# A hybrid trunk layer on one core: long lists of small score products handed to TensorE in pieces of 32, shorter turns of small work, two head pairs split for the output projection at an earlier event

## The chip, the cores and the metric

The kernel runs on one core of one Trainium2 chip. The metric is the device time of one execution in microseconds (us), as the median of three runs. All inputs and the output are fp32.

## The reference

One layer of a decoder trunk, 512 tokens of width 2048 behind 16 learned meta tokens, so T = 528. The input is RMS-normalised and multiplied by one combined projection `w_in`; its columns feed three mixers on separate heads, and the gated outputs go through one output projection `w_out`, a residual and a last RMSNorm. Cut to what matters here:

```python
proj = rms_norm(x, norm_w) @ w_in        # dq dk dv dz db da | gq gk gv gz gl | fq fk fv fz ff
# DeltaNet, 6 heads x 128, chunks of 64: (I + A) sol = rhs, A strictly lower triangular
a_mat = where(strict, einsum('bhncd,bhnsd->bhncs', kb, kc) * decay, 0)
sol = triangular_solve(eye + a_mat, rhs, lower=True)
# GLA, 5 heads (dk 64, dv 128), chunks of 64, a decay for each key dimension:
dec = exp(where(causal, g[i] - g[j], -inf))
attn = einsum('bhid,bhjd,bhijd->bhij', q, k, dec)
o = q_dec @ state + attn @ v
# forgetting attention, 5 heads x 128: softmax(q.k + c_t - c_s) @ v in blocks of 128 queries
out = rms_norm(x + concat(o_dn, o_gla, o_fox) @ w_out, final_norm_w)
```

## The kernel before, in words

**The work.** Every fp32 operand is split into a high and a low part (names ending in h and l, or beginning with h and l: `xh`/`xl`, `hbfz`/`lbfz`), and a product is three matmuls: high by high, low by high, high by low. Four stages follow each other on TensorE (PE). Most of `w_in` is multiplied first, two 128-column blocks at a time by a seven-product scheme (PSUM tiles `px`). Then come the columns of the queries and gates of GLA and of the forgetting attention, one block of 48 heavy matmuls of 512 columns each (`pbgq`, `pbfq`, `pbgz`, `pbfz`); this is the stage in which the three mixers do their own work. Then the output projection: its first part in plain products (`po`, operands `ho` and `lo` from `w_out`, `oh` and `ol` from the heads), its second by the seven-product scheme (`ps`) for the head pairs kp in `STK = (3, 4, 6, 7)`, and last the rest and the norm.

**The order.** Nothing is left to a run-time scheduler. A class `Weave` (from line 235) records the program in one order and pins it on every engine. Every piece of work is a Python generator (a chain) which yields one operation, a list of PE operations, a request for a buffer (`Get`) or events to wait for. `run` keeps a model of each engine's time and takes the chain whose next operation could start first, priority added. A list is emitted whole: nothing comes between its products. On PE a rule of turns stands above this: operations are light (the mixers' small products) or heavy (the projections); a light turn goes on while its modelled time with the next list stays below `LIGHT`, a heavy turn lasts at least `HEAVY`, if the other kind has something ready. A DMA is issued on SP's queue when the modelled DMA time is less than `BACK[t > BT]` ahead; `BACK` has one value for the first 100 us and one for the rest. Since all instructions are emitted by one helper, they all carry its line, L283; tiles tell them apart.

**GLA's score products.** GLA has five heads in three pairs p = 0, 1, 2 (the last has one head). A chunk's lower triangle is computed in levels: `gla_levels` (line 1365) makes, for the groups of levels (64, 32), (16, 8), (4, 2) and (1, 0), one list of products into PSUM tiles `pss` (one for each head of the pair), and yields it in one go. With two heads the lists have 24, 64, 64 and 64 products, with one head half of that. Each fp32 product is two matmuls in the trace, so a list of 64 is 128 matmul records. `level_operands` makes the factors: `gd` from the cumulated gates `ggc` by DVE and an exponential on ACT, then `kx = gkT * gd` and `qx = gqT * gd` on DVE. When a list is done, its masked result is taken over into `a` by DVE (COPY_PREDICATED with the mask `lmk`) and the bank is given back.

**DeltaNet's small products.** `levels` (line 1102) inverts the 64 x 64 triangles of three heads (a group g = 0 or 1) from 32 x 32 blocks: a list of 24 products of `an` and `uc` into `pm`, a copy to `m1`, a list of 48 products of `xc` and `m1`. `xc` is loaded on SP's queue from a scratch tile `sc`; `uc` is its transpose by DVE.

**Other names.** `gst` is GLA's state, `pkd` its products and gkd's transposes; `pfa`, `pfd`, `fp`, `fsm` are scores and probabilities of the forgetting attention, `pfw` its output, whose last product needs `mh` and `ml`, the two parts of a small matrix taken from `pfw` (`ml` by DVE); `pvf` and `pvgv` transpose values that were loaded to `fv` and `vgv`. `kT`, `qT` and `spgq`, `spfq` are DeltaNet's and the others' spilled rows, `rfq`, `rgz`, `rfz` raw weights.

**Head pairs of the output projection.** `seven_heads` (line 1740) splits the two finished heads of pair kp in `STK` into parts and forms their sums; it waits for `e_d`, the end of the mixers' work, unless kp is in `EARLY_KP`, where it waits for the end of GLA (`e_gla`) and the finished head 10 and takes its buffers from the pool `w_s` or `d_s`. `seven_operands` (line 1816) splits the weights for the same products.

Of the kernel before, what the change touches and what calls it, by code (L numbers as in the profile page):

```python
# [8 lines left out]
F32 = mybir.dt.float32  # L9
# [9 lines left out]
P = 128  # L19
D = 2048  # L20
KT = D // P
NM = 16
S = 512
# [5 lines left out]
NN = NB * H  # L29
# [52 lines left out]
STP, IP = 0.0, 0.05  # L82
GP, KX = (), 5
AP, KA, XP, GAP = -0.2, 2, 0.3, 0.1
BACK, BT = (3.0, 1.5), 100.0
LIGHT, SLACK, DMAL, STL = 2.0, 0.25, 1.1, 2.5
HEAVY, NEAR = 1.5, 0.05
KW = 2
NXP, SQP, NSL = -0.6, 0.0, 1.5
LP, LSL = 0.1, 1.0  # L90
WP, AOP, HDP = 1.0, -0.6, 0.0
EARLY_KP = ()
STK, KOS, OS0, OSN, OSP = (3, 4, 6, 7), 3, 1, 2, 0.1


# [265 lines left out]
def tile_hybrid_trunk(ctx, tc, xT, xtok, mtok, w_gate, w_first, w_in, w_out, consts, lmask, fin_w, out):  # L361
# [3 lines left out]
    V, A, G, PE, SP = (Engine(k, e) for k, e in zip("VAGPS", (nc.vector, nc.scalar, nc.gpsimd, nc.tensor, nc.sync)))  # L365
# [165 lines left out]
    zs, spill = {}, {}  # L531
    dzs = [drp.tile([H, P, S], F32, name=f"dzs{g}") for g in range(2)]
    e_sp, e_bank = {}, {}
    sp_of = lambda key: e_sp.setdefault(key, Ev())

    def silu_row(z, key, dst):
        if key[0] == "dz" or key in EARLY:
            yield A.activation(z, z, AF.Silu)
            yield SP.dma_start(out=dst, in_=z)
            return  # L540
        t = yield Get(row_s, f"st{key[0]}{key[1]}")
        yield V.tensor_scalar_max(t[:, :S], z, LOW)
        yield A.activation(t[:, :S], t[:, :S], AF.Exp, scale=-1.0)
        yield A.activation(t[:, :S], t[:, :S], AF.Ln, bias=1.0)
        yield A.activation(t[:, :S], t[:, :S], AF.Exp, scale=-1.0)
        yield VT(out=z, in0=z, in1=t[:, :S], op=ALU.mult)
        row_s.give(t)
        yield SP.dma_start(out=dst, in_=z)
# [174 lines left out]
    def token_rows(key, c, u):  # L723
# [29 lines left out]
    other_pairs = [(("gk", 0), ("gk", 1)), (("gv", 0), ("gv", 1)), (("gv", 2), ("gv", 3)), (("gv", 4), ("gk", 2))] \  # L753
        + [(("fk", h), ("fv", h)) for h in range(FOX_HEADS)]
    PAIRS = [p for c in zip(conv_pairs, other_pairs) for p in c]
    xpart = lambda k0, s: tuple((lambda j, t=t: t[k0 + j][:, s]) for t in (xh, xl))
    tpart = lambda d, s: tuple((lambda j, w=w: d[j // 2][w][:, j % 2, s]) for w in range(2))
    RHS = {1: xpart(0, L), 2: xpart(8, L), 3: xpart(8, R), 4: tpart(tb_, L), 5: tpart(ta, L), 6: tpart(tb_, R),
# [9 lines left out]

    pairs = [Pair(i) for i in range(len(PAIRS))]

# [67 lines left out]
    def store(p, n, u):  # L838
        yield VT(out=u, in0=u, in1=rstd, op=ALU.mult)
        key = p.keys[n]  # L840
        if key[0] in CONV:
            c = yield Get(row_s, f"cv{p.i}{n}")
            yield from conv(u, key, c, u)
            if key[0] != "dv":
                yield spilled(key, c)
            W.go(token_rows(key, c, u), -0.1, f"rows{key[0]}{key[1]}", 3.0)
        else:
            yield spilled(key, u)
            sp_of(key).set()

    CONV = {"dq": 0, "dk": DN_HEADS, "dv": 2 * DN_HEADS}
# [18 lines left out]
    EARLY = [(k[:2], int(k[2])) for k in EORD.split()]  # L870
# [231 lines left out]
    def levels(g):  # L1102
        s = gs[g]
        an, xc, xm, um = s.an, s.xc, s.xm, s.um
        uc = yield Get(m_s, f"uc{g}", (P, NN, 32))
        yield V.transpose(uc.rearrange("p n c -> p (n c)"), xc.rearrange("p n c -> p (n c)"))
        pm = yield Get(bank_s, f"pm{g}")
        p3 = pm[:, : NN * 32].rearrange("p (n c) -> p n c", c=32)
        lh = [(slice(64 * q, 64 * q + 32), slice(64 * q + 32, 64 * q + 64)) for q in range(2)]
        yield [PE.matmul(p3[lo_, n, :], an[hi_, n, lo_], uc[hi_, n, :], start=True, stop=True)  # L1110
               for n in range(NN) for lo_, hi_ in lh]
        m1 = yield Get(m_s, f"m1{g}", (P, NN, 32))
        for q in range(2):
            yield A.copy(m1[64 * q : 64 * q + 32], p3[64 * q : 64 * q + 32])
        W.go(state0(g), 0.0, f"state{g}")
        yield V.transpose(um.rearrange("p h c -> p (h c)"), xm.rearrange("p h c -> p (h c)"))
        e_um[g].set()
        yield [PE.matmul(p3[a, n, :], l[lo_, n, :], r[lo_, n, :], start=True, stop=True)
               for n in range(NN) for lo_, hi_ in lh for a, l, r in ((lo_, xc, m1), (hi_, m1, xc))]
        l1 = yield Get(m_s, f"l1{g}", (P, NN, 32))  # L1120
        yield A.copy(l1, p3)
        bank_s.give(pm)
        m_s.give(m1)
        s.uf = uf = yield Get(big_s, f"uf{g}", (P, NN, P))
        yield G.memset(uf, 0.0)
        for r in range(4):
            c = slice(32 * r, 32 * r + 32)
            yield A.copy(uf[c, :, c], uc[c])
        m_s.give(uc)
        for q in range(2):  # L1130
            yield V.tensor_copy(uf[64 * q : 64 * q + 32, :, 64 * q + 32 : 64 * q + 64], l1[64 * q : 64 * q + 32])
# [233 lines left out]
    def gla_levels(p, group, sets, pair, at, a32, ev):  # L1365
        ne = pair[0]
        ready = evs(*group)
        for s in group:
            W.go(level_operands(p, s, sets, pair, ready[s]), GPRI, f"lev{p}{s}")
        ops = dict(zip(group, (yield tuple(ready.values()))))  # L1370
        pss = yield from many(Get(bank_s, f"pss{p}{group[0]}{e}") for e in range(ne))
        mm, at_ = [], {}
        off = 0
        for s in group:
            _, kx, qx = ops[s]
            n = s if s > 16 else 32
            at_[s] = off
            for b in range(NB):
                for r in range(P // (2 * n) if s > 16 else 4):
                    k0 = b * P + r * (2 * n if s > 16 else n)  # L1380
                    q0 = k0 + n if s > 16 else k0
                    o0 = 2 * n * r if s > 16 else n * r
                    for e in range(ne):
                        rr = slice(64 * e, 64 * e + 64)
                        mm.append(PE.matmul(pss[e][o0 : o0 + n, off + b * n : off + b * n + n], kx[rr, k0 : k0 + n],
                                            qx[rr, q0 : q0 + n], start=True, stop=True))
            off += NB * n
        yield mm
# [144 lines left out]
    e_head = evs(*range(KT))  # L1533
# [4 lines left out]
    ST = STK  # L1538
# [158 lines left out]
    ORDER = (1, 2, 6, 5, 7, 3, 4)  # L1697
# [17 lines left out]
    e_d = Ev()  # L1715
# [24 lines left out]
    def seven_heads(kp):  # L1740
        i = 2 * kp
        got = yield (e_z[i], e_z[i + 1])
        yield (e_gla, (e_z if 5 in ST else e_head)[10]) if kp in EARLY_KP else e_d
        hs = (w_s, d_s) if kp in EARLY_KP else d_s
        h, l = [], []
# [68 lines left out]
                    s.src[kp, n].set(t)  # L1814

    def seven_operands():
        yield tuple(e_head[2 * kp] for kp in ST)
        for s in SEV:
            for n in ORDER:
                for kp in ST:  # L1820
                    src = yield s.src[kp, n]
                    hi = yield Get(d_s, f"wh{s.cp}{kp}{n}", (P, S), F32R)
                    lo = yield Get(d_s, f"wl{s.cp}{kp}{n}", (P, S), F32R)
                    yield A.copy(hi, src)
                    yield VT(out=lo, in0=src, in1=hi.bitcast(F32), op=ALU.subtract)
                    give(src, r_s, d_s)
                    s.op[n, kp].set((hi, lo))
# [271 lines left out]
```

## Time and profile before

| | us |
|---|---|
| three runs | 970.83, 973.27, 974.09 |
| their median | 973.27 |
| the profiled execution | 971.76 |
| its span on the core | 970.0 |
| busy: PE (matmul) | 947.7 |
| busy: DVE | 750.5 |
| busy: ACT | 569.6 |
| px from, to | 93.0, 490.0 |
| pbgq/pbfq/pbgz/pbfz beside the mixers from, to | 475.4, 782.8 |
| po's and ps's stage from, to | about 783, 950.6 |

The profiled execution's own time is 1.76 us more than its span. Times in the trace count from the span's start. "PE" is the matmul itself and "PEld" the weight load in front of it, which overlaps the matmul before. A row of the timeline gives the start of a run of like matmuls, the time until the last of them ended, the tile and its operands, the count, and in brackets the idle time ahead of it with what ended it. A releaser "issue" means that no semaphore and no transfer that the profile shows was waited for. Matmuls are pipelined, so one row's time overlaps the next row's start; the pitch between starts is what a matmul costs. In a table of stretches ("windows") the columns are the stretch, its length, the busy time of PE, PEld, DVE, ACT and POOL with the instructions begun in it, the granted TensorE clock (1.00 is full), the DMA engines' mean busy share and GB/s.

### The profile page before, as it was taken

The numbers are of one execution on the slowest core, as the hardware profiler recorded it, in microseconds if no ns is written. First come the engines' busy times: TensorE is split into PE (matmuls) and PEld (weight loads), VectorE is DVE, ScalarE is ACT, GpSimd is POOL, SyncE is SP. The second block draws the span as 40 slices with busy tenths as digits, with TensorE's granted clock in tenths as the row PEclk, the third lists the DMA queues.
The fourth block names the chain that finished last, engine by engine and source line by source line (L and its number), as shares of the span: only waits on it lengthen the run. The fifth ranks groups of instructions, "written<-read, shape, count | busy, mean of one in ns | idle before, by whom it ended". The sixth has DMA issues, their size and how long they took to land.

```text
span 970.0 us, 19077 instructions
## 1 busy us (share of the span) xinstructions
PE 947.7 (98%) x7283; PEld 844.5 (87%) x7283; DVE 750.5 (77%) x1337; ACT 569.6 (59%) x1205; POOL 67.1 (7%) x118
## 2 busy tenths in 40 slices
PE   9999999999999999999999999989989999999996
PEld 7888999999999999999987997778777787888885
DVE  7986887888888888798973666876866966888775
ACT  7865566667766576654424684637546565345445
POOL 0000101010100101110001111010010100000000
PEclk9999999999999999999999999999999999999999
DMA  9933648658784768692288335423233365474424
GB/s 344 372 113 132 164 136 226 191 150 228 193 228 117 220 154 253 171 229 83 89 290 292 97 88 182 141 85 137 99 100 135 107 207 182 154 261 153 151 67 173
DMA packets 92143, 167.18 MB, mean 172 GB/s; under 512 B 16253, under 2 KB 36477, under 8 KB 92052
## 3 DMA queue, kind: packets, MB, share of 16 engines
q1 hardware_dynamic: 87156, 157.31, 49.2%
q0 software_dynamic: 4608, 8.39, 6.5%
q8 instruction: 57, 0.93, 0.4%
q14 instruction: 34, 0.28, 0.1%
q10 hardware_dynamic: 288, 0.27, 0.1%
HBM read 142.33 MB, written 40.39 MB: 188 GB/s over the span
## 4 chain that ended last, share of the span: by engine, by line
PE 90%; DVE 3%; ACT 3%; issue 1%; DMA 1%; POOL 0%; SPq 0%; DVEq 0%; ACTq 0%; POOLq 0%
PE px L283 38%; PE po L283 9%; PE ps L283 8%; PE pz L283 5%; PE pbfq L283 5%; PE pbfz L283 5%; PE pbgz L283 4%; PE pbdz L283 2%; PE pbgq L283 2%; PE pg L283 1%; PE pss L283 1%; PE pfa L283 1%; PE pks L283 1%; PE pfw L283 1%; PE pgo L283 1%
## 5 line engine op out<-in xcount | busy, mean ns | idle before, releaser
L283 DVE SCALAR_TENSOR_TENSOR lp<-a,hp 128x1024 fp32r<-128x1024 f32 x90 | 110.7, 1231 | 36.9 <-ACT hp L283 36.1
L283 ACT CAST hp<-a 128x1024 fp32r<-128x1024 f32 x90 | 94.5, 1050 | 73.3 <-PE px L283 48.0
L283 PE MATMUL px<-xh,hp 128*128 128x264 f32 x432 | 123.7, 286 | 0.0
L283 PE MATMUL px<-xh,lp 128*128 128x264 f32 x432 | 122.7, 284 | 0.0
L283 PE MATMUL px<-xl,hp 128*128 128x264 f32 x432 | 122.7, 284 | 0.0
L283 PE MATMUL px<-tah,hp 128*128 128x264 f32 x288 | 83.8, 291 | 0.0
L283 PE MATMUL px<-tbh,hp 128*128 128x264 f32 x288 | 82.5, 287 | 0.0
L283 PE MATMUL px<-tbh,lp 128*128 128x264 f32 x288 | 82.3, 286 | 0.0
L283 PE MATMUL px<-tbl,hp 128*128 128x264 f32 x288 | 82.0, 285 | 0.0
L283 PE MATMUL px<-tah,lp 128*128 128x264 f32 x288 | 82.0, 285 | 0.0
L283 PE MATMUL px<-tal,hp 128*128 128x264 f32 x288 | 81.8, 284 | 0.0
L283 PEld LDWEIGHTS px<-xh,hp 128*128 128x128 f32 x432 | 81.4, 188 | 0.1
L283 PEld LDWEIGHTS px<-xh,lp 128*128 128x128 f32 x432 | 81.3, 188 | 0.0
L283 PEld LDWEIGHTS px<-xl,hp 128*128 128x128 f32 x432 | 81.2, 188 | 0.0
L283 PEld LDWEIGHTS px<-tbh,hp 128*128 128x128 f32 x288 | 54.3, 189 | 0.1
L283 PEld LDWEIGHTS px<-tah,hp 128*128 128x128 f32 x288 | 54.2, 188 | 0.1
L283 ACT CAST hp<-s 128x1024 fp32r<-128x1024 f32 x36 | 37.8, 1051 | 28.0 <-PE px L283 19.2
L283 PEld LDWEIGHTS px<-tal,hp 128*128 128x128 f32 x288 | 54.3, 188 | 0.0
L283 PEld LDWEIGHTS px<-tbl,hp 128*128 128x128 f32 x288 | 54.2, 188 | 0.0
L283 PEld LDWEIGHTS px<-tah,lp 128*128 128x128 f32 x288 | 54.2, 188 | 0.0
L283 PEld LDWEIGHTS px<-tbh,lp 128*128 128x128 f32 x288 | 54.2, 188 | 0.0
L283 DVE SCALAR_TENSOR_TENSOR lp<-s,hp 128x1024 fp32r<-128x1024 f32 x36 | 44.0, 1221 | 7.9 <-ACT hp L283 7.9
(406 smaller groups left out, 2642.2 us busy)
## 6 DMA issues: line engine op xcount, KB each, us to landing
a<-in_w_in SPq DMA_DIRECT2D x72, 512.0 KB, 5.7
osum<-in_w_out SPq DMA_DIRECT2D x32, 256.0 KB, 5.0
o<-in_w_out SPq DMA_DIRECT2D x16, 512.0 KB, 3.5
kd<-osum SPq DMA_DIRECT2D x25, 256.0 KB, 3.8
kd<-in_w_out SPq DMA_DIRECT2D x21, 256.0 KB, 4.2
rgz<-in_w_in SPq DMA_DIRECT2D x10, 512.0 KB
rfq<-in_w_in SPq DMA_DIRECT2D x10, 512.0 KB, 3.2
rfz<-in_w_in SPq DMA_DIRECT2D x10, 512.0 KB, 3.2
```

Of the source, the lines that this page charges most:

```text
L283: self.pin(op.call(*op.a, **op.kw))
```

## The change

`gla_levels` yields its list in pieces of `CH = 32` products, and `levels` yields its two lists in pieces of `CD = 32`; between two pieces the recorder may put other work on PE. `LIGHT` goes from 2.0 to 1.5, the second value of `BACK` from 1.5 to 3.0. `EARLY_KP` becomes (3, 4), and `seven_operands` now begins after `e_d` and waits for the heads' events at the first product (`NOP = 0`). The diff also adds hooks that stay without effect (`EXTRA` is empty, so no pair is inserted and `store`'s new branch is never reached).

```diff
-BACK, BT = (3.0, 1.5), 100.0
-LIGHT, SLACK, DMAL, STL = 2.0, 0.25, 1.1, 2.5
+BACK, BT = (3.0, 3.0), 100.0
+LIGHT, SLACK, DMAL, STL = 1.5, 0.25, 1.1, 2.5
...
+EXTRA = ()
+NOP, CH, CD = 0, 32, 32
...
-EARLY_KP = ()
+EARLY_KP = (3, 4)
...
     # levels(g)
-        yield [PE.matmul(p3[lo_, n, :], an[hi_, n, lo_], uc[hi_, n, :], start=True, stop=True)
-               for n in range(NN) for lo_, hi_ in lh]
+        mm = [PE.matmul(p3[lo_, n, :], an[hi_, n, lo_], uc[hi_, n, :], start=True, stop=True)
+              for n in range(NN) for lo_, hi_ in lh]
+        for i in range(0, len(mm), CD):
+            yield mm[i : i + CD]
...
+        for i in range(0, len(mm), CD):
+            yield mm[i : i + CD]
...
     # gla_levels(p, group, ...)
-        yield mm
+        for i in range(0, len(mm), CH):
+            yield mm[i : i + CH]
...
     # seven_operands()
-        yield tuple(e_head[2 * kp] for kp in ST)
+        yield e_d
         for s in SEV:
             for n in ORDER:
+                if n == ORDER[NOP]:
+                    yield tuple(e_head[2 * kp] for kp in ST)
```

The instructions of PE stay the same (7283 matmul records in the trace before, counting an fp32 product as two); their order changes. Turns of light work between heavy matmuls, counted in the two orders, go from 73 to 76. All instructions carry L285 afterwards, since two lines were added above the helper.

**First place, PE, the first GLA pair's last two lists** (`pss`; products from `qx` and `kx` close the levels (4, 2), those from `gkT` are the levels (1, 0)). Before, the list (1, 0) stands whole, 64 products in a row, between score products `pfa`, `pfd` of the forgetting attention:

```order
L283 MATMUL pss_7522<-qx_6892,kx_6877 32x32
L283 MATMUL pfa_7538<-fk_7012,fq_7014 128x144
L283 MATMUL pfa_7539<-fk_7012,fq_7014 128x272
L283 MATMUL pfa_7540<-fk_7012,fq_7014 128x400
L283 MATMUL pss_7630<-qx_6892,gkT_6917 32x32
...
L283 MATMUL pss_7631<-gqT_6918,gkT_6917 32x32
L283 MATMUL pfa_7541<-fk_7012,fq_7014 128x400
L283 MATMUL pfd_7542<-fk_7012,fq_7014 128x128
```

Now:

```order
L285 MATMUL pss_7674<-qx_6882,gkT_6917 32x32
L285 MATMUL pbfz_7540<-xh_171,hbfz_1_7541 128x512
L285 MATMUL pbfz_7540<-xl_172,hbfz_1_7541 128x512
L285 MATMUL pbfz_7540<-xh_171,lbfz_1_7542 128x512
L285 MATMUL pbfz_7540<-xh_176,hbfz_1_7541 128x512
L285 MATMUL pbfz_7540<-xl_177,hbfz_1_7541 128x512
L285 MATMUL pbfz_7540<-xh_176,lbfz_1_7542 128x512
L285 MATMUL pss_7673<-gqT_6918,gkT_6917 32x32
```

The first 32 products of the list stand ahead of the six heavy matmuls shown, the second 32 behind them; the lists (16, 8) and (4, 2) of this pair and of the second are cut in the same way, with six heavy matmuls between the halves (and at one place transposes of `fp` too). The `pfa` and `pfd` products stand further up now. The second pair's last list is the exception: its two pieces follow each other without anything between, behind `pfw` products.

**Second place, DVE, the first operands of the output projection** (`lo_0`, `lo_1`: low parts of the first two 1024-column pieces of `w_out`). Before, what stands between them is the forgetting attention's and the gate's work:

```order
L283 SCALAR_TENSOR_TENSOR lo_0_9240<-o_0_9061,ho_0_9239 128x1024
L283 SCALAR_TENSOR_TENSOR ol_9227<-kd_6178,oh_9219 128x512
...
L283 TENSOR_TENSOR pl_8945<-pfa_8953,ph_8851 128x128
L283 TENSOR_SCALAR fp_8982<-fp_8982,fsm_8983 128x512
L283 TENSOR_TENSOR zfz_9319<-pbfz_9173,rstd 128x512
L283 TENSOR_SCALAR stfz_9325<-zfz_9319 128x512
L283 SCALAR_TENSOR_TENSOR lo_1_9318<-o_1_9192,ho_1_9317 128x1024
```

Now the third GLA pair's factors and accumulations stand behind `lo_1`, up to the next piece `lo_2`:

```order
L285 SCALAR_TENSOR_TENSOR lo_1_9173<-o_1_9068,ho_1_9172 128x1024
...
L285 SCALAR_TENSOR_TENSOR kx_6874<-gkT_8056,gd_9010 128x8x32
L285 SCALAR_TENSOR_TENSOR qx_6882<-gqT_8057,gd_9010 128x8x32
L285 TENSOR_TENSOR fvl_9015<-pvf_9018,fvh_9014 128x512
L285 SCALAR_TENSOR_TENSOR gd_9250<-ggc_8831 128x16x16 x2
L285 SCALAR_TENSOR_TENSOR gd_9251<-ggc_8831 128x32x8 x2
L285 SCALAR_TENSOR_TENSOR kx_6874<-gkT_8056,gd_9250 128x16x16
...
L285 SCALAR_TENSOR_TENSOR kx_6894<-gkT_8056,gd_9251 128x32x8
L285 SCALAR_TENSOR_TENSOR lo_2_9282<-o_2_9121,ho_2_9281 128x1024
```

On PE the third pair's four lists (24, 64, 64 and 64 matmul records) accordingly stand amid the first `po` products, where before they stood amid the last two `pbfz` blocks; the head of the forgetting attention that stood amid the first `po` products before has come forward in exchange.

**Third place, SP's queue, the load of `xc` for DeltaNet's first group.** Before:

```order
L283 DMA sc_121<-ab 102x1024
L283 DMA rfq_5929<-in_w_in 128x1024
L283 DMA an_5917<-ans_119 128x1536
L283 DMA spgq_5968<-qgq_5965 128x512
L283 DMA xc_5939<-sc_121 128x12x32
```

Now:

```order
L285 DMA sc_121<-ab 102x1024
L285 DMA an_5886<-ans_119 128x1536
L285 DMA rfq_5936<-in_w_in 128x1024
L285 DMA kT_5938<-spdk_1998 128x528
L285 DMA kT_5938<-spdk_2260 128x528
L285 DMA xc_5925<-sc_121 128x12x32
```

Two loads of `kT` (270 KB each) stand ahead of `xc` and the store `spgq` (262 KB) behind it.

More of the change, by code (lines that the diff above doesn't have):

```diff
@@ L534, in tile_hybrid_trunk, with silu_row @@
     sp_of = lambda key: e_sp.setdefault(key, Ev())
-    def silu_row(z, key, dst):
-        if key[0] == "dz" or key in EARLY:
+    def silu_row(z, key, dst, early=False):
+        if early or key[0] == "dz" or key in EARLY:
             yield A.activation(z, z, AF.Silu)
@@ L755, in tile_hybrid_trunk @@
     PAIRS = [p for c in zip(conv_pairs, other_pairs) for p in c]
+    for i, p in EXTRA:
+        PAIRS.insert(i, p)
     xpart = lambda k0, s: tuple((lambda j, t=t: t[k0 + j][:, s]) for t in (xh, xl))
@@ L840, in store @@
         key = p.keys[n]
-        if key[0] in CONV:
+        if key[0] in ("gz", "fz"):
+            spill[key] = drp.tile([P, S], F32, name=f"sp{key[0]}{key[1]}")
+            yield from silu_row(u[:, NM:], key, spill[key], True)
+            sp_of(key).set()
+        elif key[0] in CONV:
             c = yield Get(row_s, f"cv{p.i}{n}")
@@ L1117, in levels @@
         e_um[g].set()
-        yield [PE.matmul(p3[a, n, :], l[lo_, n, :], r[lo_, n, :], start=True, stop=True)
-               for n in range(NN) for lo_, hi_ in lh for a, l, r in ((lo_, xc, m1), (hi_, m1, xc))]
+        mm = [PE.matmul(p3[a, n, :], l[lo_, n, :], r[lo_, n, :], start=True, stop=True)
+              for n in range(NN) for lo_, hi_ in lh for a, l, r in ((lo_, xc, m1), (hi_, m1, xc))]
+        for i in range(0, len(mm), CD):
+            yield mm[i : i + CD]
         l1 = yield Get(m_s, f"l1{g}", (P, NN, 32))
```

## The prediction

> **What bounds the kernel now.** I read the page first: the span, the share of each engine, the chain that ended last.
>
> ```profile
> span 970.0 us, 19077 instructions
> ...
> PE 947.7 (98%) x7283; PEld 844.5 (87%) x7283; DVE 750.5 (77%) x1337; ACT 569.6 (59%) x1205; POOL 67.1 (7%) x118
> ...
> q8 instruction: 57, 0.93, 0.4%
> ...
> PE 90%; DVE 3%; ACT 3%; issue 1%; DMA 1%; POOL 0%; SPq 0%; DVEq 0%; ACTq 0%; POOLq 0%
> ```
>
> PE is busy for 98% of the span and no matmul is added or removed, so the change can only touch the 22 us in which PE idles, the time that a matmul takes at the granted clock, and the cost of going from one kind of work to the other. Next I asked what PE waited for:
>
> ```profile
> PE pss L283 <- issue: 5.1, 3, 2.6
> PE pfw L283 <- DVE ml L283: 2.0, 3, 1.3
> PE pkd L283 <- DVE gst L283: 1.9, 2, 1.1
> ```
>
> The largest entry names no partner: three times PE stood still inside a list of GLA score products and waited for nothing that the profile shows. The timeline has the places: first a list that ran through, then the three that didn't.
>
> ```profile
> 632.12 0.39 PE L283 MATMUL pbfq<-xl,hbfq 128*128 128x512 f32 x1
> 632.35 0.40 PE L283 MATMUL pbfq<-xh,lbfq 128*128 128x512 f32 x1
> 632.67 1.29 PE L283 MATMUL pss<-qx,kx 64*32 64x32 f32 x128
> 633.89 0.33 PE L283 MATMUL pvf<-ident,fv 128*128 128x128 f32 x1
> ```
>
> ```profile
> 639.71 1.29 PE L283 MATMUL pss<-qx,kx 64*32 64x32 f32 x128
> ...
> 642.62 0.72 PE L283 MATMUL pss<-qx,gkT 64*32 64x32 f32 x62
> ...
> 646.24 0.59 PE L283 MATMUL pss<-gqT,gkT 64*32 64x32 f32 x36 [2.64 <-issue]
> ```
>
> ```profile
> 713.23 0.28 PE L283 MATMUL pss<-qx,kx 64*32 64x32 f32 x11 [0.98 <-issue]
> ...
> 720.73 0.43 PE L283 MATMUL pss<-gqT,gkT 64*32 64x32 f32 x34 [1.49 <-issue]
> ```
>
> A list of 128 records takes 633.89 - 632.67 = 1.22 us, 9.5 ns a record, so PE consumes instructions far faster there than in heavy work. They come in blocks: q8 brought 57 packets of 0.93 MB / 57 = 16 KB. That PE stops at a block's border is seen in the counts between the stalls:
>
> ```profile
> 646.24:713.23 66.99, 64.53 (x632) 51.98 (x633) 50.24 (x145) 41.88 (x117) 7.08 (x15) 0.97 0.31 104
> 713.23:720.73 7.50, 6.01 (x127) 4.75 (x128) 4.05 (x11) 2.85 (x7) 0.00 (x0) 1.00 0.46 143
> ```
>
> Between the second and the third stall lie 127 matmuls, between the first and the second 632 = 5 x 126.4. So a block is some 127 matmuls with their weight loads. In a pss list a block lasts 1.2 us, in heavy work 127 x 0.23 = 29 us (0.23 is the pitch of heavy rows, 632.12 to 632.35). The first stall is the longest because its packet came late: in the view of 640 to 647 the DMA engines are full for the first 3.5 us, and the one q8 packet falls behind that.
>
> ```profile
> DMA  9989999799999989999746100000000000100000
> ...
> q8 instruction: 1, 0.02, 0.8%
> ```
>
> The Trainium skill, "Runtime: NRT & Kernel Launch", section "Instruction fetch mechanics", says that an engine's next 16 KiB page of 256 instructions is prefetched and that crossing a border is mostly hidden, which speaks against this change. The three stalls at a distance of 126 to 127 matmuls disagree with it for lists this dense.
>
> Two of the stalls have a second cost, which the stretches behind them show:
>
> ```profile
> 646.20:649.70 3.50, 3.46 (x43) 2.60 (x44) 2.37 (x12) 1.52 (x6) 0.00 (x0) 0.54 0.01 2
> 650.00:654.00 4.00, 4.00 (x27) 3.52 (x27) 2.84 (x11) 3.38 (x10) 1.27 (x3) 1.00 0.03 5
> 721.30:724.80 3.50, 3.50 (x10) 2.74 (x10) 1.57 (x6) 2.23 (x6) 0.00 (x0) 0.54 0.02 5
> ```
>
> The granted clock is 0.54 for 3.5 us behind the stalls of 2.64 and 1.49 us, and 1.00 again in the stretch after. At 0.54 a stretch does 3.5 x 0.54 = 1.9 us of full-clock work: 1.6 us lost each. Behind the stall of 0.98 us nothing comparable stands (713.23 to 720.73 has 1.00).
>
> The Trainium skill, "TensorE: Matmul & The Clock Gate", Part 1, has the clock halved only after an idle window of about 3.4 us. By that rule stalls of 2.64 and 1.49 us would cost no clock, and the sum below would lack the 3.2 us that it takes back for it; the 0.54 above says that here they do.
>
> **The change part by part.** The sum goes against the profiled execution, 971.8 us (span 970.0 and 1.8 around it), 1.5 below the median of the three runs.
>
> *Issue stalls, -5.1.* The lists (16, 8) and (4, 2) of the first two pairs and (1, 0) of the first are cut in halves of 64 records with six heavy matmuls between. A block then holds about 64 to 110 list records and one or more groups of heavies: 0.6 to 1.0 us plus at least 6 x 0.23 = 1.4 us, so 2 us and more where it was 1.2. Counting blocks of 127 through the new order, all but two last longer than 5 us. I take all three stalls as gone. Bounds: 0 if the fetch is late anyway, -5.1.
>
> *Clock windows, -3.2.* Two of 1.6. They go with the stalls; bounds 0 and -3.2.
>
> *What stays uncut, +1.0.* The second pair's last list still stands whole in one block with pfw products behind it. Bounds: 0 (the list at 632.67 ran through) and 1.49 + 1.6 = 3.1 (the list stalled at 720.73, with its window); I take the middle row, 0.98, since half of the block's neighbours are now slow work.
>
> *Turns, +0.8.* The cost of a turn is read at a list that already has 64 records:
>
> ```profile
> 765.32 0.40 PE L283 MATMUL pbfz<-xh,lbfz 128*128 128x512 f32 x1
> 765.64 0.76 PE L283 MATMUL pss<-qx,kx 64*32 64x32 f32 x64
> 766.33 0.33 PE L283 MATMUL pfa<-ident,fp 128*128 128x128 f32 x1
> 766.42 0.47 PE L283 MATMUL pbfz<-xh,hbfz 128*128 128x512 f32 x1
> 766.73 0.39 PE L283 MATMUL pbfz<-xl,hbfz 128*128 128x512 f32 x1
> ```
>
> The last heavy matmul's pitch before the list is 0.32 instead of 0.23, the 64 records take 0.69 instead of half of 1.22, the first heavy pitch behind is 0.31: 0.09 + 0.08 + 0.08 = 0.25 us. Three turns more make 0.8. Bounds: 0.2 (one turn) and 2.0 (eight: the cuts counted without those that replace a turn elsewhere).
>
> *Data waits that the new order gives more time, -3.1.* Three waits stand where the order now has more work ahead of the waiting product.
>
> ```profile
> 518.68 0.95 PE L283 MATMUL pm<-uc,an 32*32 32x32 f32 x48 [0.68 <-DVE uc L283]
> ...
> 623.27 0.71 PE L283 MATMUL pkd<-vt,kdt 128*128 128x128 f32 x4 [1.08 <-DVE gst L283]
> ...
> 820.15 0.50 PE L283 MATMUL pfw<-ph,fvh 128*128 128x512 f32 x1 [1.31 <-DVE ml L283]
> ```
>
> The first gets three heavies more, 0.69 us; the second a heavy turn with 24 heavies and transposes; the last pfw 18 heavies instead of 9, 2.1 us. Each cover exceeds the wait, and their sum is 0.68 + 1.08 + 1.31. What is late next there is the new order's own, so the bounds are -3.1 and 0.
>
> *Data waits that the new order makes, +2.4.* Two places. SP issues two loads of kT (2 x 270 KB) ahead of xc; behind xc are queued xm and the DeltaNet loads, and PE's first `pm` list waits for it through `uc`.
>
> ```profile
> 512.00:545.00 33.00, 32.32 (x495) 25.47 (x495) 15.91 (x38) 19.46 (x39) 5.19 (x9) 1.00 0.77 238
> ```
>
> At 238 GB/s 540 KB take 2.3 us, an upper bound, since spgq (262 KB) now follows. The other place is the third GLA pair beside the first `po` products: a list whose factors come late stops PE and all heavies behind it. Prices in the rivals. I take 2.4 for both, as much as the two longest data waits of before together (1.31 + 1.08), because they arose in the same way; bounds 0 and the rival's 18.0.
>
> *No term.* The `EARLY_KP` splits are DVE and ACT rows that finish ahead of `ps`, whose products stand behind `po` and are unmoved on PE; cover: the whole `po` stretch. DeltaNet's list of 24 is one piece as before, its 48 become 32 and 16: inside the turns' count. `BACK` only moves issues; what it moves ahead of what is the kT case.
>
> Sum: 971.8 - 5.1 - 3.2 + 1.0 + 0.8 - 3.1 + 2.4 = 964.6.
>
> **The rivals.**
>
> *A: the fetch isn't relieved.* Six heavies between the halves may be too few, if what delays a block is when its packet is asked for and how full the DMA engines are (the first stall), and not only the speed of consumption. For: the packet's delay behind other transfers is untouched. Against: the list at 632.67 ran through, so the margin is near. Stalls, windows and the uncut list stay as they are: 971.8 + 0.8 - 3.1 + 2.4 = 971.9, no change to speak of. By the fetch rule of the Trainium skill named above, nothing is to be gained from shorter lists, which is this case.
>
> *B: the third pair starves the output projection, and it gets slower.* Its factors now stand on DVE among the weights' low parts:
>
> ```profile
> L283 DVE SCALAR_TENSOR_TENSOR lo<-o,ho 128x1024 fp32r<-128x1024 f32 x14 | 17.1, 1221 | 8.2 <-ACT ho L283 8.2
> ...
> L283 DVE SCALAR_TENSOR_TENSOR gd<-ggc 128x256 f32<-128x256 f32 x39 | 15.6, 430 | 0.0
> L283 DVE SCALAR_TENSOR_TENSOR qx<-gqT,gd 128x256 f32<-128x256 f32 x21 | 8.8, 418 | 0.1
> ...
> L283 DVE SCALAR_TENSOR_TENSOR kx<-gkT,gd 128x256 f32<-128x256 f32 x18 | 7.9, 437 | 0.6 <-PE pss L283 0.4
> ```
>
> ```profile
> 783.00:823.00 40.00, 38.69 (x186) 30.91 (x184) 26.34 (x74) 23.02 (x64) 1.63 (x2) 1.00 0.58 193
> 823.00:862.00 39.00, 39.00 (x170) 31.58 (x169) 34.03 (x58) 15.74 (x24) 0.00 (x0) 1.00 0.56 178
> ```
>
> A list needs some two gd, a kx and a qx: 2 x 0.43 + 0.42 + 0.44 = 1.7 us of DVE; stuck behind one low part (1.22) it is 2.9 late or PE waits for `lo` as long. Each such wait is above 1.49 and so brings a window: 2.9 + 1.6 = 4.5. Without the 2.4 the sum is 962.2; three late lists of four make 962.2 + 13.5 = 975.7, four 980.2. Above 973.27 + 2.9 it comes only with all four, so 980.2 is the time I give it. Against it: DVE has 13.7 us free of 40 in this stretch, and in the next one it is busy 34 of 39 while PE waits for nothing.
>
> *C: xc comes late.* 2.3 us at `pm` and a window of 1.6 above the sum without the 2.4: 962.2 + 3.9 + half of B's single list, 2.2 = 968.3. For: DMA share 0.77 there, and `uc` was waited for already. Against: the heavies before `pm`.
>
> **How the numbers follow.** Forecast 964.6: 0.55. A, 971.9: 0.19. B, 980.2: 0.13. C, 968.3: 0.13. About 0.3% (2.9 us) is what a measurement of this kernel can tell from no change, so "same" is 970.4 to 976.2. Faster: the forecast but 0.02, C's 0.10, a fifth of A (some stalls relieved, 0.04): 0.67. Slower: B's 0.11 and 0.02 of A: 0.13. Same: the rest, 0.20. The range begins at the sum without new waits and without the uncut list's, 964.6 - 2.4 - 1.0 = 961.2, less the spread of the runs below their median (2.4): 958.8, and ends at 971.9 plus the whole spread of the runs (3.3): 975.2. It leaves out B and little else.
>
> **What would show it right or wrong.** Right: the row "pss, issue" falls from 5.1 to 1.5 or less, no stretch of 3.5 us at a granted clock near 0.54 stands in 640 to 730, and the cut halves appear as rows of x64 of 0.7 us with heavies at 0.23 between. A shows as issue rows inside the halves, at block borders 127 matmuls apart. B shows as `pss`, `po` waiting for DVE between 783 and 823 with a clock below 1; C as `pm` waiting for `uc` by more than 2 us. The forecast is wrong if the issue row is gone and the time is not: then the turns or new data waits are dearer than their rows here.

## The result, and the profile after

| | before | after |
|---|---|---|
| median of 20 runs, us | 973.79 | 969.71 |
| lowest, highest | 970.29, 981.57 | 968.0, 972.96 |
| profiled execution, its span | 971.76, 970.0 | 969.82, 968.0 |

The ratio is 0.9959, with an interval of 0.9944 to 0.9974. It is faster by 0.4%, where 0.9% was forecast: the right side, and less than half of the size. The page of the changed kernel, its span, its busy engines and its chain:

```profile
span 968.0 us, 19091 instructions
...
PE 948.3 (98%) x7283; PEld 843.6 (87%) x7283; DVE 751.3 (78%) x1337; ACT 567.9 (59%) x1205; POOL 66.8 (7%) x118
...
PE 87%; DVE 5%; ACT 4%; DMA 2%; issue 1%; POOL 0%; DVEq 0%; SPq 0%; ACTq 0%; POOLq 0%
```

PE bounds it as before, with 3% less of the chain and more of DVE and ACT in it. What PE waited for after the change:

```profile
PE pfa L285 <- DVE fp L285: 3.1, 3, 1.3
PE pkd L285 <- DVE gst L285: 1.4, 2, 1.0
...
PE pfw L285 <- DVE ml L285: 1.1, 2, 0.5
PE pss L285 <- issue: 1.1, 1, 1.1
PE pkd L285 <- DVE gkd L285: 1.0, 1, 1.0
...
PE pm L285 <- DVE uc L285: 0.4, 1, 0.4
```

The issue row has fallen from 5.1 to 1.1, as the prediction asked for. But a row stands on top that before had not: transposes of the softmax block `fp` wait for DVE, 3.1 us. The timeline of the first pair's last list shows both, the halves at 0.69 us each (646.73 to 647.42), and the new wait a little behind:

```profile
646.73 0.76 PE L285 MATMUL pss<-qx,gkT 64*32 64x32 f32 x64
647.42 0.50 PE L285 MATMUL pbfz<-xh,hbfz 128*128 128x512 f32 x1
...
649.00 0.76 PE L285 MATMUL pss<-gqT,gkT 64*32 64x32 f32 x64
649.69 0.50 PE L285 MATMUL pbfz<-xh,hbfz 128*128 128x512 f32 x1
...
651.95 0.63 PE L285 MATMUL pfa<-ident,fp 128*128 128x128 f32 x4 [1.30 <-DVE fp L285]
```

The one issue stall left isn't in the list that stayed whole, but in a list of the third pair, which has one head and so 64 records without any cut, amid the output projection:

```profile
801.87 0.45 PE L285 MATMUL pss<-gqT,gkT 64*32 64x32 f32 x28
803.37 0.25 PE L285 MATMUL pss<-gqT,gkT 64*32 64x32 f32 x4 [1.05 <-issue]
```

The stretches in which the clock had been halved have it full now (column 1.00):

```profile
620.00:660.00 40.00, 37.34 (x592) 28.78 (x591) 29.06 (x92) 20.96 (x66) 3.69 (x7) 1.00 0.36 113
700.00:740.00 40.00, 38.42 (x581) 29.85 (x580) 25.69 (x63) 17.89 (x39) 4.34 (x10) 1.00 0.37 120
```

So both losses that the forecast named went from the profile, and most of what they were worth was spent again.

### The profile page after: what moved, and what is told of

It is laid out like the page before. It is cut to its first block, busy times and chain, and to the rows that moved or that the text cites. A ratio compares the mean times of both kernels' runs of the same rounds, so it can differ in the third digit from the quotient of the medians.

```text
span 968.0 us, 19091 instructions
## 1 busy us (share of the span) xinstructions
PE 948.3 (98%) x7283; PEld 843.6 (87%) x7283; DVE 751.3 (78%) x1337; ACT 567.9 (59%) x1205; POOL 66.8 (7%) x118
## 4 chain that ended last, share of the span: by engine, by line
PE 87%; DVE 5%; ACT 4%; DMA 2%; issue 1%; POOL 0%; DVEq 0%; SPq 0%; ACTq 0%; POOLq 0%
PE px L285 36%; PE po L285 9%; PE ps L285 8%; PE pz L285 6%; PE pbfz L285 5%; PE pbgz L285 4%; PE pbfq L285 4%; PE pbdz L285 2%; PE pks L285 2%; PE pfa L285 2%; PE pfw L285 1%; PE pg L285 1%; PE pss L285 1%; PE pbgq L285 1%; DMA sc<-ab 1%
## 5 line engine op out<-in xcount | busy, mean ns | idle before, releaser
L285 DVE SCALAR_TENSOR_TENSOR lp<-a,hp 128x1024 fp32r<-128x1024 f32 x90 | 111.2, 1236 | 36.3 <-ACT hp L285 35.9
L285 ACT CAST hp<-a 128x1024 fp32r<-128x1024 f32 x90 | 94.4, 1049 | 71.0 <-PE px L285 45.1
L285 PE MATMUL px<-xh,hp 128*128 128x264 f32 x432 | 123.7, 286 | 0.0
L285 PE MATMUL px<-xh,lp 128*128 128x264 f32 x432 | 122.7, 284 | 0.0
L285 PE MATMUL px<-xl,hp 128*128 128x264 f32 x432 | 122.7, 284 | 0.0
L285 PE MATMUL px<-tah,hp 128*128 128x264 f32 x288 | 83.9, 291 | 0.0
L285 PE MATMUL px<-tbh,hp 128*128 128x264 f32 x288 | 82.4, 286 | 0.0
L285 PE MATMUL px<-tbh,lp 128*128 128x264 f32 x288 | 82.3, 286 | 0.0
L285 PE MATMUL px<-tbl,hp 128*128 128x264 f32 x288 | 82.0, 285 | 0.0
L285 PE MATMUL px<-tah,lp 128*128 128x264 f32 x288 | 82.0, 285 | 0.0
L285 PE MATMUL px<-tal,hp 128*128 128x264 f32 x288 | 81.7, 284 | 0.0
L285 PEld LDWEIGHTS px<-xh,hp 128*128 128x128 f32 x432 | 81.4, 188 | 0.0
L285 PEld LDWEIGHTS px<-xl,hp 128*128 128x128 f32 x432 | 81.2, 188 | 0.0
L285 PEld LDWEIGHTS px<-xh,lp 128*128 128x128 f32 x432 | 81.2, 188 | 0.0
L285 ACT CAST hp<-s 128x1024 fp32r<-128x1024 f32 x36 | 37.8, 1051 | 28.3 <-PE px L285 19.5
L285 PEld LDWEIGHTS px<-tbh,hp 128*128 128x128 f32 x288 | 54.3, 189 | 0.1
L285 PEld LDWEIGHTS px<-tah,hp 128*128 128x128 f32 x288 | 54.3, 188 | 0.1
L285 PEld LDWEIGHTS px<-tal,hp 128*128 128x128 f32 x288 | 54.3, 188 | 0.0
L285 PEld LDWEIGHTS px<-tbl,hp 128*128 128x128 f32 x288 | 54.2, 188 | 0.0
L285 PEld LDWEIGHTS px<-tah,lp 128*128 128x128 f32 x288 | 54.2, 188 | 0.0
L285 PEld LDWEIGHTS px<-tbh,lp 128*128 128x128 f32 x288 | 54.1, 188 | 0.0
L285 DVE SCALAR_TENSOR_TENSOR lp<-s,hp 128x1024 fp32r<-128x1024 f32 x36 | 44.0, 1222 | 9.5 <-ACT hp L285 9.4
```

The source lines that it names most:

```text
L285: self.pin(op.call(*op.a, **op.kw))
```

## The experiments

The ratios are against runs of the kernel before on the same chip. "Lead" is the second value of `BACK`.

| run | lists | lead | median us | ratio, interval |
|---|---|---|---|---|
| the change | halves | 3.0 | 969.71 | 0.9959, 0.9944 to 0.9974 |
| e1_uncut | whole | 3.0 | 962.81 | 0.9907, 0.9882 to 0.9932 |
| e5_back_only | whole | 3.0 | 962.78 | 0.9890, 0.9863 to 0.9916 |
| e6_late_lead | whole | 3.0 from 470 us on | 966.15 | 0.9914, 0.9884 to 0.9945 |
| e2_back15 | halves | 1.5 | 969.87 | 0.9969, 0.9953 to 0.9985 |
| e9_cut_alone | all cut | 1.5 | 968.84 | 0.9957, 0.9938 to 0.9976 |
| e10_cut_and_lead | all cut | 3.0 | 972.23 | 0.9990, 0.9976 to 1.0003 |
| e3_light2 | pieces in one turn | 3.0 | 967.21 | 0.9942, 0.9926 to 0.9959 |
| e7_ch16 | 96 and 32 records | 3.0 | 975.01 | 1.0021, 1.0000 to 1.0042 |
| e16_two_cuts | two lists cut | 3.0 | 966.31 | 0.9930, 0.9908 to 0.9952 |
| e13, e14, e15 | whole | 2.2, 4.5, 6.0 | 976.16, 973.79, 975.97 | 1.0023, 0.9995, 1.0030 |

### Parts of the change undone

**e1_uncut**: `NOP, CH, CD = 0, 1000, 1000`.

> The changed kernel with its lists whole again (CH = CD = 1000); LIGHT, BACK and EARLY_KP stay changed. Theory (the gain is the fetch stalls and the half clock behind them): issue stalls inside pss come back, 3 to 6 us, with one or two stretches of 3.4 us at half clock, and the time is that of the kernel before, 972 to 975. Rival (the gain comes from the longer DMA lead or the order of the rest): no slower than the change, 969 to 970.5.

962.81 us: the theory on which the prediction rests fell at once. With the lists whole again the kernel is 6.9 us faster than the change, and 128 records in a row hardly stall:

```profile
PE pfw L285 <- DVE ml L285: 1.6, 2, 1.3
...
PE pss L285 <- issue: 0.8, 1, 0.8
```

**e2_back15**: `BACK, BT = (3.0, 1.5), 100.0` in the changed kernel.

> The changed kernel with the DMA lead of before (second value of BACK 1.5); lists in halves, turns short. Theory: stalls gone as in the change (issue under 1.5 us, no half clock) and 968 to 970.5; if the lead of 3.0 costs something ahead of the mixers' stage, up to 1 us less than the change. Rival (the longer lead is what gains): 972 to 975.

969.87, in the theory's range: with `LIGHT` and `EARLY_KP` changed as well, halves do gain at the old lead. Issue was 1.4, all of it in one stall, and that inside a half list: at 641.83, after 42 of its 64 records, with the DMA engines 0.02 busy in the 4 us before its fetch packet.

**e3_light2**: `LIGHT` 2.0 in the changed kernel.

> The changed kernel with LIGHT 2.0: the lists are handed over in pieces, but in the recorded order both halves of a 64-product list follow each other in one turn (128 records in a row at six places, as before). Theory (the separation by heavy matmuls counts, not the handing over): issue stalls of 3 to 6 us and half clock are back, 972 to 975. Rival (the place of the lists relative to other work, the third pair's above all, makes the gain, since that place is nearly that of the change): 969 to 970.5.

967.21, below both expectations and 2.5 us below the change's median, though the two intervals overlap. Its lists of the first two pairs stand as 128 records in a row, no issue row is left at all, and one window of half clock stands at 667. Whole lists need not stall, then, and at this lead the gain doesn't need the halves apart.

**e5_back_only**: the kernel before with

```diff
-BACK, BT = (3.0, 1.5), 100.0
+BACK, BT = (3.0, 3.0), 100.0
```

> The kernel before with one edit, the second value of BACK 1.5 to 3.0. New theory after the uncut run (the longer DMA lead carries the whole gain and the cuts take part of it back; LIGHT and EARLY_KP do nothing): 962 to 964, issue under 1.5 us, no half clock, no wait for fv or vgv. Rival (the gain of the uncut run needs EARLY_KP as well): 966 or more.

962.78, the same as e1, so on whole lists `LIGHT` and `EARLY_KP` together change nothing that these runs can tell, and this one number carries more than the whole gain. The first row is from its waits, the others from its timeline: two lists of 128 run through (638.68 to 639.90; 62, four single records and 62 from 643.65 to 644.87).

```profile
PE pss L283 <- issue: 0.2, 1, 0.2
```

```profile
638.68 1.29 PE L283 MATMUL pss<-qx,kx 64*32 64x32 f32 x128
639.90 0.33 PE L283 MATMUL pfa<-ident,fp 128*128 128x128 f32 x1
...
643.65 0.72 PE L283 MATMUL pss<-qx,gkT 64*32 64x32 f32 x62
...
644.21 0.73 PE L283 MATMUL pss<-gqT,gkT 64*32 64x32 f32 x62
644.87 0.44 PE L283 MATMUL pfa<-ident,fp 128*128 128x128 f32 x2
```

Like e1, it beats both kernels.

### The cut by itself

The next three kernels have a rule in `run` of the kernel before:

```diff
+            ops = c[3]
+            if c[5].startswith("levs") and len(ops) >= 48:
+                for o in ops[:32]:
+                    self.emit(o)
+                ops = ops[32:]
...
+                for _ in range(2):
...
+                        for o in mm[3]:
+                            self.emit(o)
```

Between the halves stand six heavy matmuls. The third pair's lists have 32 products and stay whole; the next expectation names them by mistake.

**e9_cut_alone**: the rule, nothing else.

> The kernel before (LIGHT 2.0, BACK 1.5, no EARLY_KP) with a rule in the recorder: of each list of 48 or more GLA products the first 32 are emitted, then six heavy matmuls, then the rest. All six lists of the first two pairs and the third pair's are cut. Theory (cutting does remove fetch stalls where they stand, and pays for it in turns and later mixer work): issue under 1.5 us, no half clock behind them, 967 to 971. Rival (what stalls is the fetch behind a DMA burst, and a half list of 64 records stalls as well): issue 3 us or more, 972 to 975.

968.84, and no issue row and no half clock: where stalls stand, cutting does remove them, as the prediction said. It gained 4.9 us of the 8.3 that they had cost in the profile.

**e10_cut_and_lead**: the rule and lead 3.0.

> The same rule with BACK 3.0: the run with BACK alone plus the cuts and nothing else. Theory (with the longer lead there is next to no stall left to remove, so a cut is pure cost): 962.8 plus nine turns at about 0.3 us and 0 to 3 us of new data waits, 965 to 969. Rival (cuts are free, the change loses by LIGHT or EARLY_KP): 962 to 964.

972.23, slower than the expected 965 to 969: it has nine more turns than e5 (78 and 69), and in its profile PE's matmuls take 3.3 us longer and PE idles 4.8 us more between the projection and the first `ps` product. That takes back nearly all that e5 gains. The largest of the new waits is again the softmax block:

```profile
PE pfa L283 <- DVE fp L283: 3.2, 3, 1.9
```

**e16_two_cuts**: the rule with `if c[5] in ("levs04", "levs01"):`, lead 3.0.

> BACK 3.0 with a cut (32 products, six heavy matmuls, the rest) in the first pair's lists (4, 2) and (1, 0) only, at the border where the late lead stalled in one execution. Theory (a cut's price is small where the order behind it stays: two turns, 0.6 us; its price in the run with all cuts was the order that it moved): the order behind these lists moves here too, so 963 to 969 by the data waits; if only turns cost, 963 to 964.

966.31: with one turn fewer than e5 (68) it is 3.5 us slower. Its profile has 1.5 us more idle time and 1.2 more of matmul time than e5's in the same stretch. Turns alone can't be the price of a cut; the new waits show that the order behind it is a part of it.

**e7_ch16**: `CH = 16` in the changed kernel.

> The changed kernel with pieces of 16 products: in the recorded order the 64-product lists stand as 96 and 32 matmul records with 3 to 9 heavy matmuls between; light turns 75 as in the change. Theory (a cut costs turns, about 0.3 us each, and the waits that the new order makes): within 2 us of the change, 968 to 971, issue under 1.5. Rival (the change's dearer part is one unlucky order, not the cuts): near the uncut run, 962 to 965.

975.01, outside both. The mixers' last product starts at 839.1 instead of the change's 822.4, so what waits for their end (`yield e_d` in `seven_operands`) comes late, and the first product of the seven-product part waits for its weight:

```profile
861.41 0.49 PE L285 MATMUL ps<-wh,oh 128*128 128x512 f32 x1 [3.90 <-ACT wh L285]
```

This is the prediction's rival B in kind, late mixers hurting the output projection, in an order with other cuts.

### Lead and luck

**e13_lead22**, **e14_lead45**, **e15_lead60**: `BACK, BT = (3.0, 2.2), 100.0` in the kernel before, and 4.5 and 6.0 in the same place.

> The kernel before with the second value of BACK at 2.2 instead of 1.5, lists whole. If a longer lead gains as such (loads issued earlier, fetches not caught behind bursts), the time lies between 963 and 973. If 3.0 gave one lucky order, anything from 962 to 976, without a trend over 2.2, 3.0, 4.5, 6.0.

> BACK's second value at 4.5, lists whole. Lead as such: no DMA waits for fv and vgv, 961 to 965. Lucky order: no relation to the lead; the issue row says which lists stall.

> BACK's second value at 6.0, lists whole. Lead as such: no DMA waits, 961 to 966, px's end 1 to 2 us later than before. Lucky order: no relation to the lead.

No trend: 973 (1.5), 976 (2.2), 963 (3.0), 974 (4.5), 976 (6.0). "A longer lead gains as such" falls too. Each order has its own incidents. In the one with 4.5, for example, no `pss` list stalls, but DeltaNet's `pm` list does, with three windows of half clock behind it:

```profile
PE pm L283 <- issue: 3.3, 1, 3.3
```

```profile
533.80:544.00 10.20, 9.78 (x83) 7.52 (x84) 1.37 (x5) 3.84 (x7) 0.41 (x1) 0.51 0.01 4
```

**e6_late_lead**: lead 3.0 only from 470 us of the recorder's time on, in the kernel before:

```diff
-                            self.t.get("D", 0.0) - BACK[self.t.get("P", 0.0) > BT] if c[3][0].dma else 0.0) + c[1], c[2]
+                            self.t.get("D", 0.0) - (3.0 if self.t.get("P", 0.0) < BT else 3.0 if self.t.get("P", 0.0) > 470.0 else 1.5) if c[3][0].dma else 0.0) + c[1], c[2]
```

> The kernel before with the lead 3.0 only from 470 us of the recorder's time on, 1.5 from 100 to 470: the order on PE is that of the run with BACK alone, SP's order in the projection stage that of before. If the longer lead costs time in the projection stage (px ended at 491.2 instead of 489.7 in the uncut run), that comes back: 0.5 to 1.5 us faster than BACK alone, 961 to 963. Rival (px's end differs from run to run): same as BACK alone.

Its runs fell into two groups, 961.4 to 961.7 and 966.2 to 968.7, and its profile is of the first; so it was profiled again.

**e12_late_lead_again**:

> The late lead once more: its runs fell into two groups, 961.4 to 961.7 and 966 to 968.7, and the profile is of the first. If this one is of the second, a window of half clock or a late load should stand in it that the first lacks.

966.55. This pair is the clearest evidence of the study: one program, two executions, with PE's order in this stage the same as in e5. In the first the list runs through:

```profile
637.71 1.29 PE L283 MATMUL pss<-qx,kx 64*32 64x32 f32 x128
```

In the second it stalls, the next list as well, and the clock is halved behind:

```profile
636.95 1.07 PE L283 MATMUL pss<-qx,kx 64*32 64x32 f32 x102
639.22 0.34 PE L283 MATMUL pss<-qx,kx 64*32 64x32 f32 x26 [1.20 <-issue]
...
646.38 0.58 PE L283 MATMUL pss<-gqT,gkT 64*32 64x32 f32 x43 [2.23 <-issue]
```

```profile
646.70:650.10 3.40, 3.40 (x27) 2.77 (x20) 2.23 (x11) 1.43 (x5) 0.00 (x0) 0.54 0.02 5
```

Issue is 3.9 us here and has no row there, and a window costs 1.6: 5.5, beside a difference of 4.9 between the two. In the first execution fetch packets start at 633.52 and 639.42, in the second at 636.31 and 644.09, which is 2.9 and 2.3 us before the two stalls end. So the same PE order runs through where its packets start early and stalls where they start late; what shifts them by 3 to 5 us (the DMA engines were 0.38 and 0.80 busy in the 4 us before the two late ones) wasn't isolated.

**e11_before_again**: the kernel before, profiled once more.

> The kernel before once more, for a second profile. If the stalls hang on where a DMA burst falls, the same three places stall again with lengths that differ by up to 1 us; issue 4 to 6 us, one or two windows of half clock.

976.26, at the upper end of its runs. The same three places stall (2.62, 0.99, 1.94; here the first), and DeltaNet's first list waits longer. Half clock stands in four windows instead of two.

```profile
648.98 0.66 PE L283 MATMUL pss<-gqT,gkT 64*32 64x32 f32 x36 [2.62 <-issue]
```

```profile
PE pm L283 <- DVE uc L283: 2.0, 1, 2.0
```

### The fetch by itself

**e4_probe**: lists of constant products added to the projection stage, all in one row and column group, with a result that nothing reads. In `mm_pair`, at seven places:

```diff
+            if j < len(sizes):
+                yield [PE.matmul(pb[:32, 32 * (i % 16) : 32 * (i % 16) + 32], ident[:32, :32], ident[:32, :32],
+                                 start=True, stop=True) for i in range(sizes[j])]
```

> The kernel before with added lists of 32x32 fp32 products of constants, into a bank that nothing reads, in the projection stage: 64, 128, 256 and 512 matmul records in a row, then 2, 4 and 8 pieces of 64 records with three px matmuls (about 0.4 us) between. Theory: 64 none, 128 at most 1 us of issue stall, 256 one stall of 1 to 2.5 us, 512 three of them, a block of 127 records apart, with half clock behind the longer ones; eight pieces of 64 (512 records as well) under 1 us in all. Rival (fetch is hidden, the stalls had another cause, such as the DMA traffic of their places): no issue stall in any of them, 512 records in 4.9 us.

No stall anywhere, but the rival isn't shown by it: the products ran one after the other, 2.14 us for 64 records, 33 ns each, so 127 records last 4.2 us, and a packet has that long to arrive. Something else showed: 512 of them kept PE busy throughout, and yet at half clock. Its row, and a stretch that is for the most part within it:

```profile
299.14 23.62 PE L283 MATMUL probe<-ident 32*32 32x32 f32 x512
```

```profile
304.60:325.10 20.50, 20.50 (x357) 20.44 (x354) 1.88 (x4) 0.00 (x0) 0.00 (x0) 0.51 0.30 99
```

**e8_probe_dense**: the same at nine places, with the groups of `pss`:

```diff
+                    e, r, col = i % 2, i // 2 % 4, 32 * (i // 8 % 16)
+                    kr, mr = slice(64 * e, 64 * e + 64), slice(32 * r, 32 * r + 32)
+                    mm.append(PE.matmul(pb[e][mr, col : col + 32], ident[kr, mr], ident[kr, mr], start=True, stop=True))
```

> The kernel before with added lists as dense as pss (products of 64 x 32 by 32 in the four column groups and two row halves, two banks that nothing reads) in the projection stage: 64, 128, 256, 512, 128, 256 records, then 4 and 8 pieces of 64 with three px matmuls between, then 256. The first probe ran at 30 ns a record, too slow to drain a block. Theory (a block of 127 records at 9.5 ns is used up before the next is there): no stall with 64, under 1 us with 128, with 256 and 512 a stall of 1 to 2.5 us at every border after the first, so 512 records take 9 to 15 us instead of 4.9; pieces of 64 between matmuls lose less than half of that. Rival (only a fetch caught behind a DMA burst stalls): 512 records in 5 to 6 us.

The single lists of 64 and 128 ran through at 9.5 to 10.8 ns a record; the list of 512 stopped three times, 128 records apart:

```profile
145.17 0.76 PE L283 MATMUL probe<-ident 64*32 64x32 f32 x64
...
287.21 1.44 PE L283 MATMUL probe<-ident 64*32 64x32 f32 x146
290.57 1.28 PE L283 MATMUL probe<-ident 64*32 64x32 f32 x128 [1.91 <-issue]
295.94 1.54 PE L283 MATMUL probe<-ident 64*32 64x32 f32 x128 [4.09 <-issue]
300.77 1.39 PE L283 MATMUL probe<-ident 64*32 64x32 f32 x110 [3.28 <-issue]
...
347.89 1.29 PE L283 MATMUL probe<-ident 64*32 64x32 f32 x128
```

It took 14.87 us instead of 4.9, with a clock of 0.51 through its last 8 us:

```profile
293.50:303.70 10.20, 4.48 (x245) 4.27 (x245) 1.22 (x1) 0.00 (x0) 0.00 (x0) 0.51 0.49 146
```

The stalls end 2.26, 2.44 and 2.41 us after the start of a fetch packet, and so do all 31 issue stalls inside lists of the eighteen profiles (2.2 to 3.0). How long a stall is depends on when the packet starts: the longest of all, 6.00 us in a list of 256, came behind DMA engines that were full for 4 us. Full engines aren't a condition: three stalls (1.39 in e2; 0.88 and 1.15 here) had them 0.02 busy or less in the 4 us before the packet. The eight pieces of 64 with three `px` between lost 1.16 + 3.81 + 1.72 = 6.7 us, against 9.3 for the 512 in a row: more than the "less than half" that was expected. Of four such pieces one stalled too (0.88).

Both probe kernels say something of the mixers' stage as well. Their lead is 1.5 and their GLA lists are whole, yet from the last `px` product to the first `ps` product they need 362.0 and 361.9 us, as little as e5 and 9.8 less than before, without an issue stall or half clock, and with 76 turns. The first one's row:

```profile
590.38:952.34 361.96, 355.78 (x3191) 292.07 (x3190) 252.65 (x642) 201.02 (x538) 29.46 (x57) 1.00 0.49 156
```

Their order there is another one again, and they come into the stage with more done (DVE is busy 252.7 us in it, 263.3 in before's), so they don't isolate a cause. But neither a lead of 3.0 nor fewer turns nor a cut is needed for so short a stage.

## Why the prediction was half right

All its terms lie between the last `px` product and the first `ps` product, 371.8 us before, 369.1 after and 362.2 in e5. (The change's last `px` product starts 1.1 us later than before's, and what follows the first `ps` product is 0.4 shorter: 0.7 us that no term covers.) I split this stretch by the starts and modelled ends of PE's matmuls: idle is where none runs. The rows of the windows give the same idle time (length less PE busy: 12.8, 10.2 and 6.05):

```profile
490.00:822.70 332.70, 319.90 (x3023) 262.15 (x3022) 229.50 (x617) 186.75 (x516) 28.32 (x56) 0.99 0.47 152
```

```profile
490.90:822.40 331.50, 321.30 (x3030) 261.95 (x3029) 231.56 (x620) 186.38 (x517) 30.16 (x57) 1.00 0.46 153
```

```profile
490.90:813.90 323.00, 316.95 (x3022) 260.83 (x3022) 228.01 (x617) 186.20 (x515) 29.39 (x57) 1.00 0.48 157
```

| us | before | after | e5 |
|---|---|---|---|
| idle, issue in pss | 5.1 | 1.05 | 0.25 |
| idle, other | 7.7 | 9.15 | 5.8 |
| matmul time | 359.0 | 358.9 | 356.2 |
| light turns | 72 | 75 | 69 |

- **Issue stalls, -5.1 and +1.0: the size was right** (5.1 to 1.05), and so was the fetch behind them, by the probe and by e9. Two things in it were wrong. The stalls weren't the cuts' to remove in this change: e1 and e5 lose nearly all of them with whole lists. And the working took the time between blocks for what decides; a list of 64 records stalled at 803.37, and a half list in e2, while the whole list of the second pair ran through. When the packet starts counts as much, and that differs between executions of one program.
- **Clock windows, -3.2: right** in the profile, none stands after.
- **Turns, +0.8: too little, and one of the two steps that failed.** Matmul time should have fallen by 3.2 with the windows gone and did not fall (359.0, 358.9), so 3.2 us were added. The three turns are 1.05 of it (pitches into and out of light work 24.38 to 26.15, less three heavy pitches of 0.24). Another 1.1 is DeltaNet's light work up to its last `pks` (42.1 to 43.2), which I had put at nothing beside `BACK`; it is the same in e1, e5 and e10, so it belongs to the lead and not to the cuts. The rest, 1.0, isn't assigned. It goes with the cutting: without half clock, matmul time is 355.8 to 356.3 in the runs with whole lists (e1, e4, e5, e6, e8; 69 to 76 turns) and 357.3 to 359.4 in those with cut ones (e2, e7, e9, e10, e16 and the change; 68 to 78 turns).
- **Data waits, -3.1 and +2.4: wrong, and the other step that failed.** Other idle time rose by 1.5 where -0.7 was forecast. The waits named did shrink (`pm` 0.68 to 0.40, the first `pkd` 1.08 to 0.42, the `pfw` at 820 gone), and so did the DMA waits for `fv` and `vgv`. But `pfa` for `fp` is new with 3.1 and `pkd` for `gkd` with 1.0, at places that I hadn't looked at. The sum treated what becomes late as two known places; with 6.9 us more than e5 (4.2 idle, 2.7 matmul time) the new order's own waits and matmul time are the larger part of the result. In sum the forecast took 7.2 us off the profiled execution and 2.0 came off: of the 5.2 missing some 2.2 are these waits, 2.3 are matmul time, and 0.7 lie outside the stretch.
- **The reference point.** The sum was made against 971.8, the lower part of the runs of before (970.3 to 976.8 but for one); e11's 976.3 has the same stalls and two windows more. Of before's medians, 972.8 to 973.8, the change takes 3 to 4 us, of the two profiles 2.0.
- **Rivals.** A as a whole is out (issue fell, the clock is full), but late packets, its reason, are what differs between e6 and e12; that transfers make them late wasn't shown. B did not come in this order: in 783 to 823 DVE was busy 29.8 of 40 us and PE idle 2.3, 1.05 of it the issue stall, but in e7 the same kind of lateness cost 3.9. C is out: `pm` waits 0.40.
- **No term for `BACK`: the largest error in reasoning.** One number carried the gain that was ascribed to the cut lists: of e5's 9.6 us in the stretch 4.9 are issue stalls and some 3.2 the half clock behind them, the very terms above. That it acts by the lead itself is refuted by e13 to e15. Which of its moves makes the order at 3.0 so good stays open: it was not undone move by move.

## What to carry to other kernels

When a planner's constant changes, cost the whole order that comes out and not the edit that gave it its name; and run each part alone, since here two parts that gain 0.4% and 1.1% alone gain 0.1 to 0.4% together. Dense lists of small products can outrun the instruction fetch, which shows as idle "issue" inside them at a constant distance in instructions; splitting them helps where they stall, and costs elsewhere. A difference of half a per cent between such orders says little about any rule that one reads into it until neighbouring values have been run.

## What the runs showed of the hardware that had not been expected

- The granted clock goes to half without idle time in the profile: at 0.51 over 20.5 us in which PE was busy 20.50 (e4), most of them with products of 32 x 32. Stalls in dense lists (2.64, 1.49 us) are followed by a window of 3.4 us, or several (10.2 us in e14).
- A fetch block is some 128 matmuls of PE with their weight loads: stalls stand 126 to 128 matmuls or a multiple apart, and the probes, with 1856 and 2368 matmuls more, fetched 72 and 76 packets of 16 KB instead of 57. A packet ahead of a stall took 0.9 to 1.4 us, and PE went on 2.2 to 3.0 us after its start. With full DMA engines ahead of it a stall reached 6.00 us.
- Two executions of one program differed by 4.9 us on one core, with these stalls and the half clock behind them as large as the difference (e6, e12).
